# Modulation vectors from row sums of products on DVE, in a two-layer diffusion transformer block

## The chip, the cores and the metric

The kernel runs on one core of a Trainium2 chip. The metric is the device time of one execution in microseconds (us). The engines are called by the profile's names: PE does matmuls (PEld loads their stationary side), DVE is the vector engine, ACT the scalar engine, POOL is GpSimd, and SP only issues transfers. Each engine works through its own queue in order; POOL and SP also issue DMA transfers.

## The reference

Two layers work on a sequence `x` of 512 tokens and a context `xc` of 256 tokens, both 1024 wide, all in float32. Each layer begins with nine modulation vectors for `x` and nine for `xc`, which shift, scale and gate its three sub-blocks:

```
def modulation(cvec, w, b):
    m = jax.nn.silu(cvec) @ w + b
    m = m.reshape(m.shape[0], 1, N_MOD, D_MODEL)     # N_MOD 9, D_MODEL 1024
    return [m[:, :, j] for j in range(N_MOD)]

mx = modulation(c, ada_w[i], ada_b[i])               # ada_w[i] is 1024 x 9216
mc = modulation(c_ctx[None, :], ada_w[i], ada_b[i])
x = x + 0.5 * mx[2] * swiglu(pre_norm(x, norm1_g[i], mx[0], mx[1]), ...)      # FFN 1; xc alike
... pre_norm(x, norm2_g[i], mx[3], mx[4]) @ w_in[i] ...                       # four mixers
x = x + mx[5] * (jnp.concatenate([ya, yd, ym, yn], axis=-1) @ w_out[i])
x = x + 0.5 * mx[8] * swiglu(pre_norm(x, norm3_g[i], mx[6], mx[7]), ...)      # FFN 2
```

`ada_w` is 37.7 MB a layer, and each of its elements is used for two products only (one for `c`, one for `c_ctx`). In the last layer `xc` leaves after the mixers, so `mc[5]` to `mc[8]` of layer 1 are not used.

## The kernel before

Activations lie transposed, features on the partitions, tokens along the row: `A` is the 512 tokens of `x`, `C` the 256 of `xc`. Every large product is three matmuls (`mm3`: high part by high part, by low part, low by high), so a weight tile `wr` is loaded by SP, rounded by ACT to `wh` and its rest taken by DVE to `wl`; there are three buffers of each. A feed-forward (`ffn`) takes 22 blocks `f` of 128 hidden features in four groups: gate and up matmuls into `guC` (for C) and `gA`, `uA` (for A), ACT's Silu, DVE's product `h`, its split into `hh` and `hl`, and after each group the down product `dacc`. The program's parts in order of time are: the start (loads, modulation vectors 0 and 1 of layer 0, norm), FFN 1 of layer 0, the mixers, the output product `wo` and FFN 2 of layer 0, FFN 1 of layer 1, and mixers, `wo` and FFN 2 of layer 1.

Vectors 0 and 1 of layer 0 are needed at once and are matmuls against `silc` (Silu of `c` and `c_ctx`), with 32 loads of 256 KB on SP. For the other sixteen (2 to 8 of layer 0, all of layer 1), `ada` is a generator that other work steps along (`fill`). For one vector and each 128-row slice `k` of the weights, POOL's queue loads two tiles `adaw` of 128x512, and DVE multiplies each by one `silc` value per partition and adds it to an accumulator `adaacc`, for two conditions: 32 instructions a vector. The contraction then still lies over the 128 partitions. Four matmuls against a block of ones (`adasum`) add them up, ACT copies the result, four PE transposes (`adatp`) turn it into columns, and DVE adds the bias (L186). `ffn` calls `self.fill(fill)` twice in a block; FFN 1 of layer 0 steps through layer 0's vectors, FFN 2 of layer 0 through layer 1's.

The order of instructions on each engine is not the order of the code: a list scheduler with a model of durations sorts them when the program is built, and each queue then runs in that fixed order.

Of the kernel before, what the change touches and what calls it, by code (L numbers as in the profile page):

```python
# [15 lines left out]
KD = 8  # L16
# [17 lines left out]
class Net:  # L34
# [43 lines left out]
    def ffn_pools(self, st):  # L78
        e = lambda n, b, s: st.enter_context(self.tc.tile_pool(name=n, bufs=b, side=s, reuse_waits="tile"))
        self.weights(e("wp", 3, self.side_x), 1024)  # L80
        self.fs = e("fs", 2, self.side_x)
        p = e("xp", 1, self.side_o)
        self.X = {q: p.tile([128, KD, t], F32, name="x" + q) for q, t in self.T.items()}
        self.hp = e("hp", 8, self.side_o)
        self.wa = e("wa", WB, self.side_o)

    def weights(self, pool, w, sets=None):

# [39 lines left out]
    def ada(self, l):  # L128

        nc = self.nc
        load = lambda q, t, k, c: q.dma_start(out=t, in_=self.I["ada_w"][l, k * 128:(k + 1) * 128, c:c + 512])  # L133
        if l == 0:
            acc = self.psum(name="adaacc")
            for k in range(KD):
                for g in range(4):
                    w = self.hp.tile([128, 768], F32, tag=("hh", "hl")[g % 2], name="adaw")[:, :512]
                    load(nc.sync, w, k, g * 512)
                    nc.tensor.matmul(acc[32 * g:32 * g + 32, :], lhsT=self.silc[:, k], rhs=w,  # L140
                                     start=(k == 0), stop=(k == KD - 1), tile_position=(0, 32 * g))
            tp = self.ada_rows(acc)
            src = tp.rearrange("p s (g r) -> p g s r", r=32)[:, :, :, 0:2]
            self.ada_bias(l, 0, src, 4)
            self.mod_cols(l, 1)
            yield
        for j in range(2 if l == 0 else 0, 9):
            acc = [self.wa.tile([128, 512], F32, tag="acc", name="adaacc", bufs=AB) for _ in range(4)]
            for k in range(KD):
                for g in range(2):  # L150
                    w = self.wa.tile([128, 512], F32, tag="wa", name="adaw")
                    if l == 0 and j == 2 and k < WB // 2:

                        nc.gpsimd.tensor_copy(w[:, 0:1], self.XNl["A"][:, KD - 1, 0:1].bitcast(F32))
                    load(nc.gpsimd, w, k, j * 1024 + g * 512)
                    for v in range(2):
                        t, c = acc[2 * g + v], self.silc[:, k, v:v + 1]
                        if k == 0:
                            nc.vector.tensor_scalar(out=t, in0=w, scalar1=c, scalar2=None, op0=ALU.mult)  # L159
                        else:  # L160
                            nc.vector.scalar_tensor_tensor(out=t, in0=w, scalar=c, in1=t, op0=ALU.mult, op1=ALU.add)  # L161
                yield
            for _ in range(AL):
                yield
            ps = self.psum(name="adasum")
# [3 lines left out]
            src = tp.rearrange("p s (g v r) -> p g s v r", g=2, v=2)[:, :, :, :, 0]  # L169
            self.ada_bias(l, j * 8, src, 2)  # L170
            self.mod_cols(l, j)
            yield

    def ada_rows(self, acc):
        nc = self.nc
# [12 lines left out]
    def mod_cols(self, l, j):  # L188

        nc = self.nc  # L190
        i = j // 3
        src = self.mods[l][:, j * 8:(j + 1) * 8]
        if j % 3 == 1:
            g = self.gains[:, 3 * l + i].rearrange("p (k o) -> p k o", o=1).to_broadcast([128, KD, 2])
            nc.vector.scalar_tensor_tensor(out=self.modAs[l][:, i], in0=src, scalar=1.0, in1=g, op0=ALU.add, op1=ALU.mult)
        elif j % 3 == 2:
            nc.vector.tensor_scalar(out=self.modGs[l][:, i], in0=src, scalar1=1.0 if i == 1 else 0.5, scalar2=None, op0=ALU.mult)

    def fill(self, n):

        for _ in range(n):
            if next(self.side, self) is self:
                return


    def unit(self, u):
# [85 lines left out]
        nc.tensor.matmul(out, lhsT=wl, rhs=xh, start=False, stop=stop)  # L292


    def ffn(self, l, i, parts, fill=0, save=(), then=None, ns=0):

        nc = self.nc
        fi = 0 if i == 0 else 1
# [3 lines left out]
        for gi, (f0, f1) in enumerate(GROUPS):  # L302
            H = []
            for f in range(f0, f1):
                W = [self.weight(up[l, fi, f, :, j], 1024) for j in range(2)]
                hh = self.hp.tile([128, 768], F32R, tag="hh", name="hh")
                hl = self.hp.tile([128, 768], F32R, tag="hl", name="hl")
                h32 = self.fs.tile([128, 768], F32, tag="h32", name="h32")
                for p in reversed(parts):
# [12 lines left out]
                    self.fill(fill)  # L322
# [50 lines left out]
def pack(inp):  # L373
# [9 lines left out]
    r["ada_w"] = a["ada_w"]  # L383
# [955 lines left out]
class Kern(Net, Mix, DN):  # L1339

    def run(self):
# [10 lines left out]
        for l in range(2):  # L1352
# [3 lines left out]
            with ExitStack() as st:  # L1356
                self.ffn_pools(st)
                if l == 0:
                    self.load_x()
                    self.side = self.ada(0)  # L1360
                    self.fill(1)
                    self.set_layer(0)
                    for u in self.units(both, NS[0] > 0):
                        for m in range(KD):
                            self.sumsq(u, m)
                    for u in self.units(both, NS[0] > 0):
                        self.norm(u, 0)
                else:
                    self.side = self.ada(1)
                    def then(u):  # L1370
                        self.fill(80)
                        self.set_layer(1)
                        self.norm(u, 0)
                    self.second_half(0, both, then)
                def then(u):
                    self.fill(80)
                    self.norm(u, 1)
                self.ffn(l, 0, both, FILL[0] if l == 0 else 0, parts, then, NS[2 * l])
            self.mixers(l, need)
        self.open_xn()  # L1380
        with ExitStack() as st:
# [4 lines left out]
    def second_half(self, l, parts, then):  # L1386
# [62 lines left out]
                    self.norm(due, 2)  # L1449
            due = u  # L1450
        self.norm(due, 2)
        self.ffn(l, 2, parts, FILL[1] if l == 0 else 0, (), then, NS[2 * l + 1])

    def mixers(self, l, need):
        tc, nc = self.tc, self.nc
# [78 lines left out]

STEPS = 1.0
PREP, NST, LAST = (2, 3), 3, 1
FILL = (2, 3)
NK = (3, 6)

_INS = ["xT", "cxT", "cT", "ada_w", "adab", "gains", "ident", "wgu", "wd", "win", "cs_swa", "cs_mla", "sink",  # L1540
        "masks", "rpbS", "rpbT", "mlag", "wuq", "wukv", "woutk0", "woutm0", "woutk1", "woutm1", "dn_m", "dn_tri", "dn_neg", "dn_i2", "convw", "dngate", "dnng"]


# [31 lines left out]
```

## Time and profile before

| | us |
|---|---|
| median of 3 runs (3255.51 to 3258.74) | 3257.91 |
| the profiled execution | 3254.35 |
| its span, first to last instruction | 3252.6 |
| PE busy in the span | 3129.6 (96%) |
| DVE busy | 1715.9 (53%) |
| ACT busy | 1069.6 (33%) |
| POOL busy | 463.6 (14%) |
| DVE's product-and-add for the modulation (L161), 448 instructions | 315.4 |

Matmuls overlap their neighbours, so a duration in the table of groups is longer than the step from one start to the next; where the text speaks of a step it means the difference of two starts. Rows are quoted as the profile prints them; L12 is line 12 of the program.

### The profile page before, as it was taken

What the parts mean: (1) busy time and instruction counts of PE and PEld (TensorE: products, weight loads), DVE (VectorE), ACT (ScalarE), POOL (GpSimd) and SP (SyncE); (2) the same over time, 40 slices, a digit from 0 to 9 for tenths busy, and PEclk for the clock granted to TensorE, in tenths of its full rate; (3) what the DMA queues carried; (4) which work ended last, traced back from release to release, by engine and by line L of the source; (5) the groups of instructions that cost most, each with busy time, mean ns of one, the idle gap of its engine ahead of it and who ended that gap; (6) DMA issues with size and microseconds to landing.
All of it is one profiled execution on the core that took longest, in us unless ns stands there. A gap on an engine that the chain in (4) does not pass through costs nothing.

```text
span 3252.6 us, 48912 instructions
## 1 busy us (share of the span) xinstructions
PE 3129.6 (96%) x19586; PEld 2713.3 (83%) x19586; DVE 1715.9 (53%) x3044; ACT 1069.6 (33%) x1927; POOL 463.6 (14%) x772
## 2 busy tenths in 40 slices
PE   7999999998999999999999999999997899999998
PEld 4888888886788889888889988888886688788887
DVE  5746354836855477675736332322746744353334
ACT  3212112555444433121224212122455353342223
POOL 2201010411232021121102000000311322000001
PEclk9999999999999999999999999999998999899999
DMA  6534242514533354454424221212523623323333
GB/s 244 153 104 138 87 117 81 168 62 124 159 91 87 89 191 131 142 153 126 128 77 123 63 64 59 72 53 67 148 78 114 162 57 81 121 86 96 97 97 104
DMA packets 135396, 357.45 MB, mean 110 GB/s; under 512 B 20000, under 2 KB 33824, under 8 KB 134912
## 3 DMA queue, kind: packets, MB, share of 16 engines
q1 hardware_dynamic: 101056, 255.47, 25.9%
q0 software_dynamic: 34112, 98.85, 11.0%
q8 instruction: 154, 2.52, 0.3%
q14 instruction: 74, 0.61, 0.1%
HBM read 316.89 MB, written 39.65 MB: 110 GB/s over the span
## 4 chain that ended last, share of the span: by engine, by line
PE 57%; DVE 4%; issue 3%; DMA 2%; ACT 1%; POOL 0%; POOLq 0%; DVEq 0%; SPq 0%; ACTq 0%
PE dacc L290 4%; PE dacc L292 4%; PE dacc L291 4%; PE gA L290 4%; PE gA L291 4%; PE uA L290 4%; PE uA L292 4%; PE uA L291 4%; PE gA L292 4%; PE guC L292 3%; PE guC L290 3%; PE guC L291 3%; PE o L740 2%; PE pj L290 1%; PE pj L292 1%
## 5 line engine op out<-in xcount | busy, mean ns | idle before, releaser
L269 ACT CAST wh<-wr 128x1024 fp32r<-128x1024 f32 (+5 forms) x443 | 394.7, 893 | 1239.4 <-PE dacc L291 453.3
L274 DVE TENSOR_TENSOR wl<-wr,wh 128x1024 fp32r<-128x1024 f32 (+5 forms) x443 | 461.2, 1043 | 422.6 <-ACT wh L269 391.6
L290 PE MATMUL dacc<-hh,wh 128*128 128x256 f32 (+1 forms) x1392 | 452.5, 326 | 2.2 <-ACT wh L269 1.9
L292 PE MATMUL dacc<-hh,wl 128*128 128x256 f32 (+1 forms) x1392 | 450.4, 326 | 3.6 <-DVE wl L274 3.5
L291 PE MATMUL dacc<-hl,wh 128*128 128x256 f32 (+1 forms) x1392 | 452.2, 326 | 0.0
L161 DVE SCALAR_TENSOR_TENSOR adaacc<-adaw,silc,adaacc 128x512 f32<-128x512 f32 x448 | 315.4, 748 | 12.2 <-DMA adaw<-ada_w 11.8
L290 PE MATMUL guC<-xnhC,wh 128*128 128x256 f32 x1056 | 300.2, 285 | 1.6 <-ACT xnhC L263 1.5
L291 PE MATMUL guC<-xnlC,wh 128*128 128x256 f32 x1056 | 299.5, 284 | 1.5 <-DVE xnlC L264 1.5
L292 PE MATMUL guC<-xnhC,wl 128*128 128x256 f32 x1056 | 299.0, 283 | 0.5 <-DVE wl L274 0.5
L290 PEld LDWEIGHTS dacc<-hh,wh 128*128 128x128 f32 x1392 | 261.4, 188 | 32.0 <-ACT wh L269 6.1
L290 PE MATMUL gA<-xnhA,wh 128*128 128x512 f32 (+1 forms) x752 | 284.8, 379 | 1.7 <-ACT xnhA L263 1.7
L292 PEld LDWEIGHTS dacc<-hh,wl 128*128 128x128 f32 x1392 | 261.0, 188 | 29.6 <-DVE wl L274 5.0
L290 PE MATMUL uA<-xnhA,wh 128*128 128x512 f32 (+1 forms) x752 | 283.0, 376 | 0.6 <-ACT wh L269 0.6
L292 PE MATMUL uA<-xnhA,wl 128*128 128x512 f32 (+1 forms) x752 | 282.8, 376 | 0.7 <-DVE wl L274 0.7
L291 PE MATMUL uA<-xnlA,wh 128*128 128x512 f32 (+1 forms) x752 | 282.9, 376 | 0.0
L292 PE MATMUL gA<-xnhA,wl 128*128 128x512 f32 (+1 forms) x752 | 282.8, 376 | 0.0
L291 PE MATMUL gA<-xnlA,wh 128*128 128x512 f32 (+1 forms) x752 | 282.2, 377 | 0.0
L291 PEld LDWEIGHTS dacc<-hl,wh 128*128 128x128 f32 x1392 | 261.4, 188 | 24.6
L133 POOL DMA_DIRECT2D adaw<-ada_w x256 | 140.6, 550 | 799.2 <-DVE adaacc L159 483.3
L348 DVE SCALAR_TENSOR_TENSOR xA<-dacc,modG,xA 128x512 f32<-128x512 f32 (+1 forms) x160 | 101.9, 640 | 239.3 <-PE dacc L292 239.2
L290 PEld LDWEIGHTS guC<-xnhC,wh 128*128 128x128 f32 x1056 | 202.7, 192 | 9.5 <-ACT wh L269 5.2
L291 PEld LDWEIGHTS guC<-xnlC,wh 128*128 128x128 f32 x1056 | 202.6, 192 | 4.4 <-DVE xnlC L264 2.0
(354 smaller groups left out, 5944.9 us busy)
## 6 DMA issues: line engine op xcount, KB each, us to landing
wr<-wgu SPq DMA_DIRECT2D x176, 512.0 KB, 3.6
adaw<-ada_w POOLq DMA_DIRECT2D x256, 256.0 KB, 3.3
wr<-wd SPq DMA_DIRECT2D x120, 320.0 KB, 3.0
wr<-wd SPq DMA_DIRECT2D x64, 384.0 KB, 3.2
wr<-win SPq DMA_DIRECT2D x44, 512.0 KB, 3.9
adaw<-ada_w SPq DMA_DIRECT2D x32, 256.0 KB, 5.2
hl<-eh SPq DMA_DIRECT2D x32, 192.0 KB, 3.0
hl<-el SPq DMA_DIRECT2D x24, 192.0 KB, 3.3
```

The costliest lines, as they stand in the source:

```text
L133: load = lambda q, t, k, c: q.dma_start(out=t, in_=self.I["ada_w"][l, k * 128:(k + 1) * 128, c:c + 512])
L161: nc.vector.scalar_tensor_tensor(out=t, in0=w, scalar=c, in1=t, op0=ALU.mult, op1=ALU.add)
L269: nc.scalar.copy(hi, src)
L274: (nc.vector if leng == "V" else nc.gpsimd).tensor_tensor(lo, src, hi.bitcast(F32), op=ALU.subtract)
L290: nc.tensor.matmul(out, lhsT=wh, rhs=xh, start=start, stop=False)
L291: nc.tensor.matmul(out, lhsT=wh, rhs=xl, start=False, stop=False)
L292: nc.tensor.matmul(out, lhsT=wl, rhs=xh, start=False, stop=stop)
L348: nc.vector.scalar_tensor_tensor(out=x, in0=acc, scalar=gate[:, i, m, r:r + 1], in1=x, op0=ALU.mult, op1=ALU.add)
L740: nc.tensor.matmul(o[:, q0 + q], lhsT=p[:, q * 128:q * 128 + 128], rhs=v(kb), start=False, stop=kb == 3 and q == n // 128 - 1)
```

## The change

The weights come from the host transposed as well (`ada_t`: 128 output features on the partitions, the 1024 inputs along the row). `crow` holds `c` and `c_ctx` as rows; SP loads them to all 128 partitions (`silr`, 128x2x1024, 1 MB written) and ACT applies Silu. One DVE instruction then multiplies a tile of 128x1024 with one condition's row, adds up along the row, starts from the bias, and leaves 128 finished values in a column of `mod`. The sums on PE, ACT's copies, the transposes and the bias adds of the sixteen vectors go. One tile is 512 KB, with four buffers in place of six of 256 KB. `fill` now takes the share of the block that is done, and the sixteen vectors are spread over three feed-forwards: 2 to 7 of layer 0 over FFN 1 of layer 0, then 8 of layer 0 and 0 to 3 of layer 1 over FFN 2 of layer 0, then 4 to 8 of layer 1 over FFN 1 of layer 1. The unused `c_ctx` vectors 5 to 8 of layer 1 are left out, so there are 224 products. Vectors 0 and 1 of layer 0 stay matmuls. The scratch that POOL's transfers use is 4096 bytes a partition.

```diff
-WB, AB = 6, 5
-AL = 3
+AB = 4
...
+        self.silr = self.const.tile([128, 2, 1024], F32, name="silr")
+        nc.sync.dma_start(out=self.silr, in_=self.I["crow"].rearrange("(o v) k -> o v k", o=1).to_broadcast([128, 2, 1024]))
+        nc.scalar.activation(self.silr, self.silr, ACTF.Silu)
...
-                    load(nc.gpsimd, w, k, j * 1024 + g * 512)
-                    for v in range(2):
-                        t, c = acc[2 * g + v], self.silc[:, k, v:v + 1]
...
-                            nc.vector.scalar_tensor_tensor(out=t, in0=w, scalar=c, in1=t, op0=ALU.mult, op1=ALU.add)
...
-            for i in range(4):
-                nc.tensor.matmul(ps[32 * i:32 * i + 32], lhsT=self.ones[:, 0:32], rhs=acc[i], tile_position=(0, 32 * i))
-            tp = self.ada_rows(ps)
...
+        for n, (l, j) in enumerate(js):
+
+            nv = 1 if l == 1 and j >= 5 else 2
+            for m in range(j * 8, j * 8 + 8):
+                w = self.wa.tile([128, 1024], F32, tag="wa", name="adaw", bufs=AB)
+                if l == 0 and n == 0 and m - j * 8 < AB:
+
+                    nc.gpsimd.tensor_copy(w[:, 0:1], self.XNl["A"][:, KD - 1, 0:1].bitcast(F32))
+                nc.gpsimd.dma_start(out=w, in_=self.I["ada_t"][l, m])
+                for v in range(nv):
+                    o = self.wa.tile([128, 1024], F32, tag="wo", name="adao", bufs=1)
+                    nc.vector.tensor_tensor_reduce(o, w, self.silr[:, v], 1.0, self.adab[:, l, m:m + 1],
+                                                   ALU.mult, ALU.add, self.mods[l][:, m, v:v + 1])
...
-    nc = bacc.Bacc("TRN2", target_bir_lowering=False, num_devices=1)
+    nc = bacc.Bacc("TRN2", target_bir_lowering=False, num_devices=1, dynamic_dma_scratch_size=4096)
```

PE, early in FFN 2 of layer 0, where the sums of layer 1's first vector stood (about 1239 us of the profile); before:

```order
L290 MATMUL guC<-xnhC,wh 128x256
L291 MATMUL guC<-xnlC,wh 128x256
L290 MATMUL uA<-xnhA,wh 128x256
L291 MATMUL uA<-xnlA,wh 128x256
L167 MATMUL adasum<-adaacc,ones 32x512 x4
L292 MATMUL guC<-xnhC,wl 128x256
L290 MATMUL guC<-xnhC,wh 128x256
```

The same place now:

```order
L286 MATMUL guC<-xnhC,wh 128x256
L287 MATMUL guC<-xnlC,wh 128x256
L286 MATMUL uA<-xnhA,wh 128x256
L287 MATMUL uA<-xnlA,wh 128x256
L286 MATMUL guC<-xnhC,wh 128x256
```

The four sums are gone, and the feed-forward's matmuls follow one another. Of PE's 18019 instructions 128 go in all, 64 sums and 64 transposes.

DVE, from the first modulation work of FFN 1 of layer 0 on (about 64 us); before:

```order
L159 TENSOR_SCALAR adaacc<-adaw,silc 128x512 x4
L327 TENSOR_TENSOR h_410<-sg,guC 128x256
L161 SCALAR_TENSOR_TENSOR adaacc<-adaw,silc,adaacc 128x512 x2
L274 TENSOR_TENSOR wl<-wr,wh 128x1024
L161 SCALAR_TENSOR_TENSOR adaacc<-adaw,silc,adaacc 128x512 x2
L327 TENSOR_TENSOR h_410<-sg,uA 128x512
```

The same place now (each product is two instructions, the row product and the read of its sum into `mod`):

```order
L160 ISA adao,mod_72<-adaw,silr,adab 128x1024
L160 ISA mod_72 128x1
L323 TENSOR_TENSOR h_413<-sg,guC 128x256
L160 ISA adao,mod_72<-adaw,silr,adab 128x1024
L160 ISA mod_72 128x1
L270 TENSOR_TENSOR wl<-wr,wh 128x1024
L160 ISA adao,mod_72<-adaw,silr,adab 128x1024
L160 ISA mod_72 128x1
L323 TENSOR_TENSOR h_413<-sg,uA 128x512
```

Two or four short instructions ahead of a block's product or weight rest became one long and one tiny one.

DVE, at the output product `wo` of layer 0 (about 1160 us; `xC`, `xA` are the closes that free its banks); before:

```order
L274 TENSOR_TENSOR wl<-wr,wh 128x1024
L161 SCALAR_TENSOR_TENSOR adaacc<-adaw,silc,adaacc 128x512 x5
L1409 SCALAR_TENSOR_TENSOR xC<-wo,modG_76,xC 128x256
L161 SCALAR_TENSOR_TENSOR adaacc<-adaw,silc,adaacc 128x512
L1409 SCALAR_TENSOR_TENSOR xC<-wo,modG_76,xC 128x256
L274 TENSOR_TENSOR wl<-wr,wh 128x1024
```

The same place now:

```order
L270 TENSOR_TENSOR wl<-wr,wh 128x1024
L1407 SCALAR_TENSOR_TENSOR xC<-wo,modG_76,xC 128x256 x2
L270 TENSOR_TENSOR wl<-wr,wh 128x1024
L1407 SCALAR_TENSOR_TENSOR xC<-wo,modG_76,xC 128x256
L1407 SCALAR_TENSOR_TENSOR xA<-wo,modG_76,xA 128x512 x3
```

The modulation work left this stage; its first product of the second batch now stands behind the norm that follows `wo`. On SP the load of `silr` stands ahead of `adab` and of the loads of `x`; the rest of SP's order is as it was.

## Rows read from the trace of the kernel before

**Rows 1.** Busy time in four stretches (stretch, length, engines, PE clock, DMA share, GB/s).
```profile
0.00:44.00 44.00, 23.53 (x85) 6.84 (x85) 12.20 (x27) 13.90 (x24) 7.52 (x13) 0.96 0.90 338
44.00:617.00 573.00, 570.07 (x3384) 496.74 (x3384) 340.94 (x537) 145.37 (x232) 91.62 (x162) 1.00 0.41 122
...
1240.00:1780.00 540.00, 540.00 (x3255) 473.98 (x3252) 335.10 (x529) 131.09 (x208) 84.64 (x141) 1.00 0.44 129
1780.00:2345.00 565.00, 561.34 (x3430) 503.18 (x3428) 209.55 (x317) 144.44 (x233) 26.90 (x39) 1.00 0.26 76
```
**Rows 2.** PE's waits for weights' rests, 44 to 608 us: total us, times, longest.
```profile
PE dacc L292 <- DVE wl L274: 0.5, 1, 0.5
```
**Rows 3.** Order of time on PE at one sum: start, length, instruction.
```profile
1239.08 0.28 PE L291 MATMUL uA<-xnlA,wh 128*128 128x256 f32 x1
1239.29 1.06 PE L167 MATMUL adasum<-adaacc,ones 128*32 128x512 f32 x8
1240.28 0.38 PE L292 MATMUL guC<-xnhC,wl 128*128 128x256 f32 x1
1240.50 0.28 PE L290 MATMUL guC<-xnhC,wh 128*128 128x256 f32 x1
```
**Rows 4.** The same at one vector's transposes.
```profile
1248.42 0.28 PE L292 MATMUL uA<-xnhA,wl 128*128 128x256 f32 x1
1248.54 0.60 PE L180 MATMUL adatp<-ident,adasb 128*128 128x128 f32 x4
...
1249.09 0.28 PE L291 MATMUL guC<-xnlC,wh 128*128 128x256 f32 x1
```
**Rows 5.** The same at the first vector's sums, issued in four pieces.
```profile
94.81 0.39 PE L291 MATMUL uA<-xnlA,wh 128*128 128x512 f32 x1
95.03 0.39 PE L292 MATMUL uA<-xnhA,wl 128*128 128x512 f32 x1
95.35 1.05 PE L167 MATMUL adasum<-adaacc,ones 128*32 128x512 f32 x2
...
96.66 0.40 PE L291 MATMUL gA<-xnlA,wh 128*128 128x512 f32 x1
```
**Rows 6.** Groups by line on PE (count, busy us, mean ns, idle before).
```profile
L167 PE MATMUL adasum<-adaacc,ones 128*32 128x512 f32 x128 | 20.2, 605 | 0.0
L180 PE MATMUL adatp<-ident,adasb 128*128 128x128 f32 x68 | 10.2, 273 | 0.7 <-ACT adasb L177 0.7
```
**Rows 7.** Groups by line and shape on DVE.
```profile
L161 DVE SCALAR_TENSOR_TENSOR adaacc<-adaw,silc,adaacc 128x512 f32<-128x512 f32 x448 | 315.4, 748 | 12.2 <-DMA adaw<-ada_w 11.8
L274 DVE TENSOR_TENSOR wl<-wr,wh 128x1024 fp32r<-128x1024 f32 x227 | 277.8, 1226 | 319.6 <-ACT wh L269 301.2 <-PE gA L292 5.6 <-PE htr L995 4.3
L327 DVE TENSOR_TENSOR h<-sg,uA 128x512 f32<-128x512 f32 x88 | 60.4, 687 | 246.7 <-PE uA L292 246.0 <-ACT sg L326 0.7
L159 DVE TENSOR_SCALAR adaacc<-adaw,silc 128x512 f32<-128x512 f32 x64 | 28.2, 481 | 5.8 <-DMA adaw<-ada_w 4.2 <-PE adasum L167 1.5
L247 DVE TENSOR_SCALAR rsv<-nsum 128x2 f32<-128x2 f32 x20 | 3.0, 152 | 1.5 <-PE nsum L233 1.3
```
**Rows 8.** ACT's wait for a free weight buffer: total us, times, longest.
```profile
ACT wh L269 <- PE gA L291: 283.2, 77, 4.7
```
**Rows 9.** Busy time in the start, columns as in rows 1.
```profile
30.00:42.00 12.00, 11.32 (x36) 2.52 (x36) 2.99 (x3) 1.46 (x2) 0.00 (x0) 0.87 1.05 411
```
**Rows 10.** A load of 1 MB in the list of DMA issues (KB, us to landing).
```profile
xA<-xT SPq DMA_DIRECT2D x2, 1024.0 KB, 6.7
```
**Rows 11.** Order of time on DVE and PE in `wo` of layer 0.
```profile
1160.84 3.40 DVE L161 SCALAR_TENSOR_TENSOR adaacc<-adaw,silc,adaacc 128x512 f32<-128x512 f32 x5
1164.15 0.48 DVE L1409 SCALAR_TENSOR_TENSOR xC<-wo,modG,xC 128x256 f32<-128x256 f32 x1
...
1165.74 0.50 PE L290 MATMUL wo<-xnhA,wh 128*128 128x512 f32 x1 [1.29 <-DVE xC L1409]
...
1166.87 0.39 PE L292 MATMUL wo<-xnhC,wl 128*128 128x256 f32 x1 [0.40 <-DVE wl L274]
```

More of the change, by code (lines that the diff above doesn't have):

```diff
@@ L84, in ffn_pools @@
         self.hp = e("hp", 8, self.side_o)
-        self.wa = e("wa", WB, self.side_o)
+        self.wa = e("wa", 1, self.side_o)
     def weights(self, pool, w, sets=None):
@@ L132, in ada @@
         nc = self.nc
[L133 to L154, printed above, removed]
-                    load(nc.gpsimd, w, k, j * 1024 + g * 512)
-                    for v in range(2):
-                        t, c = acc[2 * g + v], self.silc[:, k, v:v + 1]
-                        if k == 0:
-                            nc.vector.tensor_scalar(out=t, in0=w, scalar1=c, scalar2=None, op0=ALU.mult)
-                        else:
-                            nc.vector.scalar_tensor_tensor(out=t, in0=w, scalar=c, in1=t, op0=ALU.mult, op1=ALU.add)
-                yield
-            for _ in range(AL):
-                yield
-            ps = self.psum(name="adasum")
-            for i in range(4):
-                nc.tensor.matmul(ps[32 * i:32 * i + 32], lhsT=self.ones[:, 0:32], rhs=acc[i], tile_position=(0, 32 * i))
-            tp = self.ada_rows(ps)
[L169 to L172, printed above, removed]
@@ new lines, in ada_first @@
+        acc = self.psum(name="adaacc")
+        for k in range(KD):
+            for g in range(4):
+                w = self.hp.tile([128, 768], F32, tag=("hh", "hl")[g % 2], name="adaw")[:, :512]
+                nc.sync.dma_start(out=w, in_=self.I["ada_w0"][k * 128:(k + 1) * 128, g * 512:(g + 1) * 512])
+                nc.tensor.matmul(acc[32 * g:32 * g + 32, :], lhsT=self.silc[:, k], rhs=w,
+                                 start=(k == 0), stop=(k == KD - 1), tile_position=(0, 32 * g))
+        tp = self.ada_rows(acc)
@@ new lines, in ada_first, with ada @@
+        src = tp.rearrange("p s (g r) -> p g s r", r=32)[:, :, :, 0:2]
+        self.ada_bias(0, 0, src, 4)
+        self.mod_cols(0, 1, 2)
+    def ada(self, js):
+        nc = self.nc
+        for n, (l, j) in enumerate(js):
[9 more added lines that the diff above has]
+                                                   ALU.mult, ALU.add, self.mods[l][:, m, v:v + 1])
+                if m == j * 8 + 7:
+                    self.mod_cols(l, j, nv)
+                yield
@@ L186, in ada_bias, with mod_cols, beside, fill @@
         self.nc.vector.tensor_tensor(dst, src, b, op=ALU.add)
-    def mod_cols(self, l, j):
+    def mod_cols(self, l, j, nv):
         nc = self.nc
         i = j // 3
-        src = self.mods[l][:, j * 8:(j + 1) * 8]
+        src = self.mods[l][:, j * 8:(j + 1) * 8, 0:nv]
         if j % 3 == 1:
-            g = self.gains[:, 3 * l + i].rearrange("p (k o) -> p k o", o=1).to_broadcast([128, KD, 2])
-            nc.vector.scalar_tensor_tensor(out=self.modAs[l][:, i], in0=src, scalar=1.0, in1=g, op0=ALU.add, op1=ALU.mult)
+            g = self.gains[:, 3 * l + i].rearrange("p (k o) -> p k o", o=1).to_broadcast([128, KD, nv])
+            nc.vector.scalar_tensor_tensor(out=self.modAs[l][:, i, :, 0:nv], in0=src, scalar=1.0, in1=g, op0=ALU.add, op1=ALU.mult)
         elif j % 3 == 2:
[L197 to L203, printed above, removed]
+            nc.vector.tensor_scalar(out=self.modGs[l][:, i, :, 0:nv], in0=src, scalar1=1.0 if i == 1 else 0.5, scalar2=None, op0=ALU.mult)
+    def beside(self, js):
+        self.side, self.sides, self.sided = self.ada(js), 8 * len(js), 0
+    def fill(self, part):
+        while self.sided < min(1.0, part) * self.sides:
+            self.sided += 1
+            next(self.side, None)
     def unit(self, u):
@@ L292, in mm3, with ffn @@
         nc.tensor.matmul(out, lhsT=wl, rhs=xh, start=False, stop=stop)
-    def ffn(self, l, i, parts, fill=0, save=(), then=None, ns=0):
+    def ffn(self, l, i, parts, save=(), then=None, ns=0):
         nc = self.nc
@@ L308, in ffn @@
                 h32 = self.fs.tile([128, 768], F32, tag="h32", name="h32")
-                for p in reversed(parts):
+                for n, p in enumerate(reversed(parts)):
                     if p == "C":
@@ L1359, in run @@
                     self.load_x()
-                    self.side = self.ada(0)
-                    self.fill(1)
+                    self.ada_first()
+                    self.beside([(0, j) for j in range(2, 8)])
                     self.set_layer(0)
@@ L1368, in run @@
                 else:
-                    self.side = self.ada(1)
+                    self.beside([(0, 8)] + [(1, j) for j in range(4)])
                     def then(u):
-                        self.fill(80)
                         self.set_layer(1)
@@ L1375, in then @@
                 def then(u):
-                    self.fill(80)
                     self.norm(u, 1)
-                self.ffn(l, 0, both, FILL[0] if l == 0 else 0, parts, then, NS[2 * l])
+                if l == 1:
+                    self.beside([(1, j) for j in range(4, 9)])
+                self.ffn(l, 0, both, parts, then, NS[2 * l])
             self.mixers(l, need)
@@ L1451, in second_half @@
         self.norm(due, 2)
-        self.ffn(l, 2, parts, FILL[1] if l == 0 else 0, (), then, NS[2 * l + 1])
+        if l == 1:
+            self.beside([])
+        self.ffn(l, 2, parts, (), then, NS[2 * l + 1])
     def mixers(self, l, need):
```

11 lines of the change are left out of this document (6 added, 5 removed).

## The prediction

> **What bounds the kernel.** I read the busy time by stretches first, then PE's waits, then the order of time on PE around the work that goes, and last the groups by line. In the three feed-forwards that carry modulation work now or after the change, PE is busy 570.07 of 573 us, 540.00 of 540 and 561.34 of 565, at a granted clock of 1.00 of 2.4 GHz [rows 1]. DVE is busy 340.94, 335.10 and 209.55 us of them, so it has 230 us to spare in the first, 205 in the second and 355 in the third. Within 44 to 608 us PE waited for a weight's rest from DVE for 0.5 us in all [rows 2]. So these stages are as long as PE's steps: an instruction taken off PE shortens them by its step, and work moved about on DVE costs nothing while weights come in time. The start is another matter: from 30 to 42 us the DMA share is full (1.05) at 411 GB/s [rows 9], and the first feed-forward begins behind these loads.
>
> **What goes from PE.** At one set of four sums, the matmuls around it start at 1239.08 and 1240.50, 1.42 us apart, with one ordinary matmul and the sums between them [rows 3]. Two ordinary steps of that shape take 0.12 us each (1248.42 to 1248.54 [rows 4]), so the set costs 1.42 - 0.24 = 1.18 us. (By busy time, 20.2 us for 128 records [rows 6], eight would be 1.26; records overlap their neighbours, so I take steps.) A vector's four transposes cost, from 1248.42 to 1249.09 with two ordinary steps in it, 0.67 - 0.24 = 0.43 us [rows 4]. The first vector of layer 0 was summed in four pieces with feed-forward matmuls between; one piece costs 96.66 - 95.03 - 2 x 0.22 = 1.19 us (a step of 512 columns is 95.03 - 94.81 = 0.22 [rows 5]), four of them 4.8 us. There are sixteen vectors (128 records of sums by 8, and 64 of the 68 transposes [rows 6]): 15 x 1.18 + 4.8 + 16 x 0.43 = 17.7 + 4.8 + 6.9 = **29.4 us off PE**. All sixteen lie in the two stages where PE has nothing to wait for, so I count all of it. Below nothing it can hardly go; the bound on this side is that PE then waits for something else (a rival below).
>
> **What DVE gets.** The trace has no row product with a sum, so I bound it. Two float32 tiles of 512 columns cost 687 ns, of 1024 columns 1226 ns, 539 for another 512; the old product with a scalar per partition costs 748 [rows 7]. One product of 1024 with such a scalar is then 748 + 539 = 1.29 us, and the read of the sum is like DVE's smallest instruction here, 0.15 [rows 7]: 1.44 us, 224 of them 323 us. The old work was 315.4 + 28.2 = 344 [rows 7], so DVE is about even. Lower bound 1.23 us; upper bound, if the stream ran at half speed, 748 + 539 + 1067 (another 1024 columns at 539 per 512 make 1.08) = 2.4, with the read 2.5. By stage: FFN 1 of layer 0 loses 28 x 0.48 + 196 x 0.75 = 160 us and gets 96 x 1.44 = 138; FFN 2 of layer 0 gets 80 x 1.44 = 115 for the larger part of 288 old instructions; FFN 1 of layer 1 gets 48 x 1.44 = 69 on top of 210, of 565. None fills.
>
> What could hurt is DVE's order: an `h`, an `hl` or a weight's `wl` queues behind a product. The cover is PE's lead. ACT mostly waits for PE to free a weight buffer, 283.2 us in 77 waits behind gate matmuls [rows 8]; from there the next up weight is needed only after 24 up matmuls of A and 24 gate matmuls of C, 24 x 0.22 + 24 x 0.12 = 8.2 us. `wl` takes 1.23 us [rows 7], ACT's rounding of the same tile I put at the same, together 2.5, so DVE may be 5.7 us late before PE feels it. Two products in front are 2.9 us now, against 1.5 us for a pair of the old ones. I take nothing for it, and 0 to 8 us as bounds; if the cover were gone, each block would lose up to 1.4 us, the difference of the pairs.
>
> [...]
>
> **The start.** `silr` is 128 x 2 x 1024 x 4 bytes = 1.05 MB ahead of the loads that bound the start; at 411 GB/s [rows 9] it moves everything behind it by **2.6 us**. All partitions read the same 8 KB, which no load here does; from below, nothing, if queues were still filling; from above, the 6.7 us that a load of 1 MB takes to land [rows 10], say 6.7. I take 2.6, since the DMA engines are the limit. ACT's Silu on `silr` comes before its squares of `x`; those are not what the stage ends with (the loads are), so I take nothing for it; it costs a few us if they were.
>
> **The output product.** In `wo` of layer 0 DVE ran five old products from 1160.84 for 3.40 us while a close of `xC` and then a `wl` stood behind them; PE idled 1.29 us for the close and 0.40 for the rest [rows 11]. Now no modulation work stands there: loads of the second batch wait for the norm behind `wo`. I take 1.5 of the 1.7 us back (bounds 0 and 2). What is late next there is the norm itself, as before.
>
> **POOL and its queue.** 128 loads of 512 KB replace 256 of 256 KB; same bytes, half the issues. In FFN 1 of layer 1 40 loads are new, 21 MB in 565 us, 37 GB/s beside 76 [rows 1], far from the 411 seen. POOL's stores of `x` come in the last group, when the products are issued. Nothing.
>
> **Sum.** -29.4 + 2.6 - 1.5 = -28.3 us. The profiled execution took 3254.35, giving 3226.1; the runs' median is 3257.91, 3.6 us above it, so I predict 3257.91 - 28.3 = **3229.6, say 3229.5 us**. Its own range is 3224 to 3235.
>
> **The rivals.**
> 1. The start is dearer, the one row read 128 times being slow: +4 us and more, 3234 to 3238. For it: no such read in the trace. Against: 1 MB loads land in 6.7 us. Chance 0.08.
> 2. [...] Chance 0.13.
> 3. The change does not do what it says: PE loses the sums but waits as long for weights, because the stage is really paced by ACT and DVE. Time 3252 to 3262. For it: DVE is at work 60% of these stages, in the same chain as the weights. Against: 0.5 us of waits [rows 2], and ACT waits for PE [rows 8], not PE for ACT. Chance 0.06.
> 4. The other side: DVE becomes the bound. In the first feed-forward its other work is 341 - 160 = 181 us, which leaves 392 for 96 products: from 4.1 us a product on, over three times my price, PE must wait. At 4.4 us it loses 96 x 0.3 = 29 us there and the gain is gone; at 5 us it loses 96 x 0.9 = 86, and the time is about 3315 even if FFN 2 loses nothing. For it: an instruction form that no row shows. Against: three rows at one column per about 1.05 ns. Chance 0.05.
> My forecast keeps 0.68.
>
> Two runs differ from no change only by more than about 0.2% (6.5 us). Forecast and rivals 1 and 2 are faster by that (0.89), rival 3 is the same (0.06), rival 4 slower (0.05). The range takes forecast, 1 and 2 with the bounds: low 3257.9 - 29.4 - 2 = 3226, less the 3.6 by which single executions lie lower and a little for the order elsewhere, 3220; high -29.4 + 6.7 + 8 = 3243.
>
> **What would show it.** Right: PE's busy time in the span falls by some 25 to 30 us; no waits over 1 us inside the feed-forwards; the first feed-forward begins 2 to 3 us later than at 44 us; products of 1.2 to 1.5 us with small reads; no modulation work on DVE in `wo`. Wrong: waits of PE for `wl` in FFN 1 of layer 0 (rival 2 or 4), a start more than 5 us later (rival 1), or other stalls in the mixers from the scheduler's new order, which I could not price and hold at a few us of either sign.

## The result

The changed kernel took **3222.69 us** (median of 4 runs, 3218.36 to 3226.16), the kernel before, on the same chip, 3256.71 (4 runs): a ratio of 0.9895, 95% interval 0.9878 to 0.9912. That is 34.0 us less, where 28.3 were forecast.

The busy time of the changed kernel by stretches, for the same stages as [rows 1] (stretch, length, then each engine, PE's granted clock, DMA share, GB/s):

```profile
0.00:46.00 46.00, 24.13 (x84) 6.64 (x84) 11.79 (x26) 15.39 (x24) 7.51 (x13) 1.00 0.93 346
46.00:604.00 558.00, 555.03 (x3283) 493.21 (x3284) 316.51 (x492) 140.78 (x222) 53.30 (x92) 0.99 0.38 117
1222.00:1759.00 537.00, 534.26 (x3210) 476.75 (x3210) 338.54 (x532) 131.87 (x207) 58.45 (x95) 1.00 0.47 145
1759.00:2323.00 564.00, 560.33 (x3429) 502.86 (x3427) 208.53 (x321) 144.88 (x234) 28.31 (x40) 1.00 0.26 77
```

PE is still the full engine, and its list is shorter; DVE's load hardly moved. Its groups by line, product and read of the sum (count, busy us, mean ns, idle before), which take the place of L161 and L159 in [rows 7]:

```profile
L160 DVE CUSTOM_DVE_ANT_0 adao<-adaw,silr,adab 128x1024 f32<-128x1024 f32 x224 | 287.1, 1282 | 11.8 <-DMA adaw<-ada_t 8.5
...
L160 DVE DVE_READ_ACCUMULATOR2_ANT mod<- 128x1 f32 x224 | 18.7, 83 | 0.0
```

A product costs 1.28 us and its read 0.08, together 1.36 where 1.44 was estimated. PE's waits in the first feed-forward of layer 0 (46 to 608 us), beside [rows 2]:

```profile
PE guC L286 <- ACT xnhC L259: 1.5, 1, 1.5
PE dacc L286 <- ACT wh L265: 1.2, 2, 0.9
PE gA L286 <- ACT xnhA L259: 0.8, 1, 0.8
PE dacc L288 <- DVE wl L270: 0.5, 1, 0.5
```

Weights' rests are as punctual as before, and the other three rows stand in the trace of before too, at 1.5, 1.7 and 0.8 us. At the start, in order of time on PE, the last transposes and the first feed-forward matmul (start, length, instruction):

```profile
44.20 0.65 PE L172 MATMUL adatp<-ident,adasb 128*128 128x128 f32 x4 [0.68 <-ACT adasb L169]
46.40 0.51 PE L286 MATMUL guC<-xnhC,wh 128*128 128x256 f32 x2 [1.55 <-ACT xnhC L259]
```

DVE's groups in `wo` of layer 0 (1128 to 1198 us) hold no product; in [rows 11] five stood in a row there:

```profile
L270 DVE TENSOR_TENSOR wl<-wr,wh 128x1024 fp32r<-128x1024 f32 (+1 forms) x12 | 11.8, 981 | 14.5 <-ACT wh L265 14.1
L1407 DVE SCALAR_TENSOR_TENSOR xA<-wo,modG,xA 128x512 f32<-128x512 f32 (+1 forms) x9 | 5.8, 660 | 12.1 <-PE wo L288 12.1
```

The table below has the length of each stage, from the start of its first matmul on PE to that of the next stage, in two traces of each kernel (the second of each comes from an experiment, `before_again` and `again`); the last columns are the difference of the two means and what the forecast said.

| stage, us | before | before_again | changed | again | difference | forecast |
|---|---|---|---|---|---|---|
| start | 43.99 | 43.86 | 46.40 | 45.36 | +2.0 | +2.6 |
| FFN 1, layer 0 | 576.58 | 578.69 | 563.83 | 563.98 | -13.7 | -14.9 |
| mixers, layer 0 | 511.85 | 515.41 | 517.38 | 513.52 | +1.8 | 0 |
| `wo`, layer 0 | 74.82 | 76.22 | 71.26 | 71.25 | -4.3 | -1.5 |
| FFN 2, layer 0 | 574.43 | 575.87 | 561.77 | 562.83 | -12.9 | -14.5 |
| FFN 1, layer 1 | 566.51 | 566.90 | 564.03 | 565.05 | -2.2 | 0 |
| mixers, layer 1 | 459.17 | 460.04 | 449.46 | 458.09 | -5.8 | 0 |
| `wo`, layer 1 | 61.74 | 61.74 | 61.20 | 61.21 | -0.5 | 0 |
| FFN 2, layer 1 | 383.50 | 382.96 | 381.28 | 381.04 | -2.1 | 0 |

### The profile page after: what moved, and what is told of

Its sections match the earlier page's. It is cut to its first block, busy times and chain, and to the rows that moved or that the text cites. A ratio compares the mean times of both kernels' runs of the same rounds, so it can differ in the third digit from the quotient of the medians.

```text
span 3216.6 us, 48071 instructions
## 1 busy us (share of the span) xinstructions
PE 3092.6 (96%) x19394; PEld 2699.5 (84%) x19394; DVE 1670.6 (52%) x2964; ACT 1061.2 (33%) x1912; POOL 391.3 (12%) x646
## 4 chain that ended last, share of the span: by engine, by line
PE 55%; DVE 3%; DMA 1%; ACT 1%; issue 1%; POOL 0%; SPq 0%; POOLq 0%; DVEq 0%; ACTq 0%
PE dacc L286 4%; PE dacc L287 4%; PE dacc L288 4%; PE uA L288 4%; PE uA L286 4%; PE uA L287 4%; PE gA L287 4%; PE gA L286 4%; PE gA L288 4%; PE guC L288 3%; PE guC L286 3%; PE guC L287 3%; PE o L738 2%; PE pj L286 1%; PE pj L288 1%; PE pj L287 1%
## 5 line engine op out<-in xcount | busy, mean ns | idle before, releaser
L160 DVE CUSTOM_DVE_ANT_0 adao<-adaw,silr,adab 128x1024 f32<-128x1024 f32 x224 | 287.1, 1282 | 11.8 <-DMA adaw<-ada_t 8.5
L288 PEld LDWEIGHTS guC<-xnhC,wl 128*128 128x128 f32 x1056 | 203.0, 192 | 1.9 <-DVE wl L270 1.5
```

The lines of the kernel that those rows point to most:

```text
L160: nc.vector.tensor_tensor_reduce(o, w, self.silr[:, v], 1.0, self.adab[:, l, m:m + 1], ALU.mult, ALU.add, self.mods[l][:, m, v:v + 1])
```

## The experiments

**1. Both kernels once more.** `again` is the changed kernel, `before_again` the kernel before, without an edit.

> The changed kernel once more, unchanged. Its one profile so far and the one of before differ by -12.8 us in the first feed-forward, -12.7 in the second feed-forward of layer 0, -3.6 in `wo` of layer 0, -2.5 in the first feed-forward of layer 1, but also by +5.5 in the mixers of layer 0 and -9.7 in those of layer 1, where the change does nothing. Theory: the feed-forwards and `wo` repeat within 1 us, because their length is PE's list of steps, and the mixers move by several us from one execution to the next. Rival: the mixers repeat too, within 1 us; then their -4.2 in sum belongs to the change, by the scheduler's new order. Time 3218 to 3227.

> The kernel before once more, unchanged, for a second trace. Theory (the mixers vary from one execution to the next and the feed-forwards do not): feed-forwards at 576.6, 574.4, 566.5 within 1 us, `wo` of layer 0 at 74.8 within 0.5, the last feed-forward at 383.5; the mixers of the two layers differ from 511.9 and 459.2 by several us, as they did between executions of the changed kernel (517.4 and 513.5; 449.5 and 458.1). Rival: the mixers repeat within 1 us.

`again` took 3226.16 us (4 runs, 3215.75 to 3228.68) against 3258.11, ratio 0.990 (0.988 to 0.992); the one run of `before_again` took 3263.44. In the table the feed-forwards repeat within about 2 us, `wo` within 1.4, and the mixers move by up to 8.6 (449.46 to 458.09). So the mixers' -5.8 and +1.8 are not to be read as the change's work. PE's granted clock differs with them in the mixers of layer 1, in two traces of one and the same kernel: first the changed kernel (stage 449.46 us, mean clock 0.93), then `again` (458.09, 0.90), by stretches as above:

```profile
2728.00:2736.00 8.00, 5.09 (x77) 4.33 (x75) 3.37 (x12) 2.16 (x5) 2.65 (x4) 1.00 0.31 74
2736.00:2747.00 11.00, 9.12 (x26) 6.03 (x27) 6.03 (x12) 3.31 (x6) 1.62 (x2) 0.53 0.60 195
2747.00:2753.00 6.00, 5.22 (x35) 4.39 (x34) 4.23 (x6) 2.98 (x7) 0.00 (x0) 1.00 0.81 254
2753.00:2768.00 15.00, 13.90 (x54) 11.67 (x55) 6.01 (x13) 6.07 (x11) 0.00 (x0) 0.54 0.13 44
```

```profile
2728.00:2738.00 10.00, 9.01 (x104) 8.04 (x103) 3.77 (x13) 3.48 (x7) 1.00 (x2) 1.00 0.33 87
2738.00:2772.00 34.00, 30.45 (x118) 24.67 (x108) 17.39 (x35) 11.85 (x20) 3.26 (x4) 0.51 0.39 124
```

In both the clock falls to its lower level (0.53, 0.54 and 0.51 in these rows) after a stretch in which PE was busy 64% and 90% of the time. At that level PE's steps are longer: in the trace of before, matmuls of 128x512 start 0.427 us apart at a clock of 0.50 (2489 to 2493 us) and 0.227 apart at 1.00 (94 to 95 us). In the first of the two it comes back after 10 us and falls once more for 14; in `again` it stays down for 34. So a mixer stage can differ by 9 us with nothing changed.

**2. The sums on PE left out, alone** (with the copy on ACT, the transposes and the bias add that follow them; the old products stay).

```diff
-            ps = self.psum(name="adasum")
             for i in range(4):
-                nc.tensor.matmul(ps[32 * i:32 * i + 32], lhsT=self.ones[:, 0:32], rhs=acc[i], tile_position=(0, 32 * i))
-            tp = self.ada_rows(ps)
-            src = tp.rearrange("p s (g v r) -> p g s v r", g=2, v=2)[:, :, :, :, 0]
-            self.ada_bias(l, j * 8, src, 2)
+                g, v = i // 2, i % 2
+                nc.vector.tensor_tensor(self.mods[l][:, j * 8 + 4 * g:j * 8 + 4 * g + 4, v], acc[i][:, 0:4],
+                                        self.adab[:, l, j * 8 + 4 * g:j * 8 + 4 * g + 4], op=ALU.add)
```

> The kernel before with the four sums on PE of each vector, their copy on ACT and the four transposes left out; what the vectors get instead is the unsummed product of each partition in four of its columns plus the bias, so the modulation vectors are not what the reference computes. All old products and loads stay, in their old order. Theory (PE's steps are the stage's length): 29.4 us less than before, ratio 0.991, with about -14.5 to -15 in each of the two feed-forwards of layer 0 and `wo` as before. Rival (the stage is paced by the weights' rest on DVE and PE's time does not carry): within 5 us of before. Second rival (sums cost more than their steps, by what they disturb around them): -34 or more.

It took 3272.20 us against 3258.11, ratio **1.0048** (1.0033 to 1.0063): slower, which neither expectation had. The first feed-forward did get shorter (564.6 us), but `wo` of layer 0 grew to 84.2 and the second feed-forward to 599.8. PE's waits from 1119 to 1275 us, the end of `wo` and the norm behind it, and the busy time in three stretches from there:

```profile
PE gA L289 <- DVE xnlA L262: 12.7, 6, 2.3
PE gA L288 <- ACT xnhA L261: 10.9, 7, 2.6
PE rb L238 <- DVE dg L234: 7.4, 1, 7.4
PE guC L288 <- ACT xnhC L261: 4.7, 2, 3.8
PE guC L289 <- DVE xnlC L262: 2.5, 1, 2.5
```

```profile
1119.00:1203.00 84.00, 73.32 (x469) 66.57 (x468) 64.28 (x105) 21.39 (x37) 30.11 (x43) 0.94 0.68 218
1203.00:1271.00 68.00, 40.37 (x221) 36.54 (x222) 68.00 (x141) 13.25 (x28) 21.83 (x39) 0.80 0.49 146
1271.00:1803.00 532.00, 529.68 (x3170) 472.05 (x3170) 281.17 (x448) 131.01 (x205) 59.16 (x95) 1.00 0.36 108
```

DVE is busy all of 68 us, PE only 40 of them, and the granted clock falls to 0.80. All five rows wait for pieces of a norm that stand behind products on DVE (48 of L161 in this `wo`, 30 in that of before). Before, an accumulator came free only when PE had summed it (L159 waits for `adasum` in [rows 7]), and the sums had their place among the feed-forward's matmuls. So I read the sums as what paced DVE: without them the products moved forward in DVE's order, into `wo` and the norm. That the move comes from this, and not from another reason for which the scheduler sorted anew, is argued; experiment 4 tests what the move costs.

**3. The changed kernel without its second gate.** In the changed kernel the first four loads of the first two batches each wait, by a small POOL copy, for the norm's `XNl`. Here only those of the first batch do.

```diff
-                if l == 0 and n == 0 and m - j * 8 < AB:
+                if l == 0 and n == 0 and j == 2 and m - j * 8 < AB:
```

> The changed kernel with the second batch's first four loads no longer tied to the norm behind `wo`, so that the first products of that batch run in `wo` of layer 0 as the old ones did. Theory (modulation work on DVE in front of closes and weights' rests costs PE waits there): `wo` of layer 0 goes from 71.3 back towards the 74.8 us of the kernel before, +1.5 to +3.5, the rest unchanged. Rival (the 3.6 us there come from the order of `wo` and the norm, not from the products): `wo` stays within 0.5 us of 71.3.

It took 3253.53 us (10 runs), ratio 0.9987 (0.9977 to 0.9997), 27.4 more than `again` on the same chip: without the gate the change gains 4.6 us. `wo` went to 77.1 and the second feed-forward to 577.7, so the expectation had the sign and the place, and the size far too small. PE's waits from 1134 to 1240 us:

```profile
PE guC L286 <- ACT xnhC L259: 5.9, 2, 4.6
PE guC L287 <- DVE xnlC L260: 2.7, 2, 2.2
PE nsum L229 <- DVE nt L256: 1.3, 1, 1.3
```

They name the same norm. The first row names ACT, whose `xnhC` needs `nt` from DVE. The rows add up to 9.9 us, of 21 that these two stages lost; from 1208 to 1233 us the granted clock has a mean of 0.73, and how the rest divides is open.

**4. The gate in the kernel before, without and with its sums.** `no_sums_gated` is experiment 2, `gate_only` the kernel before, each with

```diff
-                    if l == 0 and j == 2 and k < WB // 2:
+                    if j == (0 if l else 2) and k < WB // 2:
```

> As the earlier kernel without the sums on PE (the vectors again get the unsummed product of each partition in four of its columns plus the bias, so they are not what the reference computes), and in addition the first three loads of layer 1's vectors wait for the norm behind `wo`, as the changed kernel's second batch does. Theory (the sums on PE also paced DVE: without them the old products crowd into `wo` and stand ahead of closes and the norm; a gate mends that, and what is left is PE's own time): `wo` of layer 0 at 71.3 us instead of 84.2, the second feed-forward at 561 to 563 instead of 599.8, the time 27 to 33 us less than before, ratio 0.990 to 0.992. Rival (the loss came from something else in that kernel, such as the small bias operations, or a product of the old kind is too slow without pacing wherever it begins): `wo` 71 to 75, but the second feed-forward stays above 580 and the time within 10 us of before.

> The kernel before, sums on PE kept, with the one addition that the first three loads of layer 1's vectors wait for the norm behind `wo`. Theory: `wo` of layer 0 falls from 74.8 to about 71.3 us, the second feed-forward stays at 574, so 3 to 4 us less in all, ratio 0.999. Rival (the gate delays the vectors so that the end of layer 0 waits for the last one): the second feed-forward or the start of the first one of layer 1 grows by 5 us or more.

`no_sums_gated` took 3236.29 us against 3257.15, ratio 0.9931 (0.9913 to 0.9949): with the gate, leaving PE's work out pays 20.9 us, `wo` is 71.26 and the first feed-forward 562.2, but the second stays at 571.1, between the two expectations. PE's steps on `gA` in it (each from one start to the next, added up) are 131.1 us against 121.7 before, so 9.4 us of what is missing lie there. `gate_only` took 3264.75, ratio 1.0015 (0.9996 to 1.0034), which can't be told from no change: `wo` fell to 71.28 as the theory had it, and the second feed-forward grew to 591.1, as the rival had it, but not for the rival's reason: matmul by matmul against the trace of before, all of the 16.6 us are lost in the first 47 us of the stage, and nothing at its end. Most of it is lost at A's norm, where DVE is full and PE's clock falls (the stretch from 1232 to 1256 us, columns as above):

```profile
1232.00:1256.00 24.00, 16.62 (x75) 14.95 (x74) 24.00 (x39) 6.45 (x10) 6.98 (x13) 0.57 0.64 186
```

DVE's order of time there, first in `gate_only`, then in the changed kernel:

```profile
1230.37 0.48 DVE L264 SCALAR_TENSOR_TENSOR xnlA<-nt,mod,xnhA 128x256 fp32r<-128x256 f32 x1
1230.76 2.73 DVE L161 SCALAR_TENSOR_TENSOR adaacc<-adaw,silc,adaacc 128x512 f32<-128x512 f32 x4
1233.41 0.47 DVE L260 SCALAR_TENSOR_TENSOR nt<-xA,modA,rb 128x256 f32<-128x256 f32 x1
1233.80 0.48 DVE L264 SCALAR_TENSOR_TENSOR xnlA<-nt,mod,xnhA 128x256 fp32r<-128x256 f32 x1
1234.20 2.73 DVE L161 SCALAR_TENSOR_TENSOR adaacc<-adaw,silc,adaacc 128x512 f32<-128x512 f32 x4
```

```profile
1222.19 0.87 DVE L256 SCALAR_TENSOR_TENSOR nt<-xA,modA,rb 128x256 f32<-128x256 f32 x2
1222.97 1.28 DVE L160 CUSTOM_DVE_ANT_0 adao<-adaw,silr,adab 128x1024 f32<-128x1024 f32 x1
1224.18 0.08 DVE L160 DVE_READ_ACCUMULATOR2_ANT mod<- 128x1 f32 x1
1224.18 0.87 DVE L260 SCALAR_TENSOR_TENSOR xnlA<-nt,mod,xnhA 128x256 fp32r<-128x256 f32 x2
```

A's norm is written in two halves of its columns, and the gate opens on a column of the first. In the second half four old products (2.73 us) stand ahead of each slice, its `nt` and its `xnlA`; of the new ones, two for two slices, 1.36 us a slice. PE's matmuls on A take these slices one after another, so the old bunch stalls them: their steps on `gA` are 131.1 us in `gate_only` too, and 124.5 in the changed kernel.

**5. The gate on the norm's last column.** `late_gate` is the changed kernel with that, in both batches; `late_gate_old` is `gate_only` with it for layer 1's vectors alone.

```diff
-                    nc.gpsimd.tensor_copy(w[:, 0:1], self.XNl["A"][:, KD - 1, 0:1].bitcast(F32))
+                    nc.gpsimd.tensor_copy(w[:, 0:1], self.XNl["A"][:, KD - 1, TX - 1:TX].bitcast(F32))
```

> The kernel before with the sums on PE kept and the first loads of layer 1's vectors tied to the last column of the norm of A (the earlier gate was its first column, which is written by the first of the norm's two column halves, so that four old products of 0.7 us stood between the pieces of the second half). Theory (the 16.6 us that the second feed-forward lost under the earlier gate were those products in front of `xnlA`, and the half clock that followed PE's waits): no product inside that norm, `wo` at 71.3, the second feed-forward at 572 to 575, the time 3 to 6 us under before, ratio 0.998 to 0.999. Rival (the loss came from the vectors being late or dense over the whole stage): the second feed-forward stays above 585.

> The changed kernel with its gate on the last column of A's norm in place of the first, in both batches. Theory (the new products in the second half of that norm cost gA steps some 2 to 3 us: 124.5 us of gA steps in the second feed-forward against 121.7 before): the second feed-forward at 559 to 561 instead of 562.4, gA steps at 121.7, the time 1 to 4 us under the changed kernel's. Rival (those waits come from the norm itself): gA steps stay at 124.5 and the time does not change.

`late_gate` took 3223.31 us against 3254.84, ratio 0.9905 (0.9886 to 0.9924). Its second feed-forward is 558.9 us, and PE's steps on `gA` in it are 121.5 us, against 124.5 in the changed kernel and 121.7 before: the theory's 3 us are there in the trace, but the whole time can't show them beside the mixers (527.3 in this trace, with 41 us at the lower clock). `late_gate_old` took 3270.51, ratio 1.0044 (1.0029 to 1.0058), so the theory failed: no product is left inside the norm, and the second feed-forward still takes 594.6. The rival had the size (above 585) and half of the reason: the vectors are late, but not over the whole stage. One row of PE's waits (1195 to 1795 us) holds 15.4 of the 20 us by which it is longer than before:

```profile
PE adasum L168 <- DVE adaacc L162: 15.4, 1, 15.4
```

The first vector's sum has its fixed place in PE's order; when the products begin later, PE stands there until DVE has added up the vector. With sums on PE the products are bound from both sides: early, they hold up the norm; late, PE waits for them. The row products end in `mod`, and PE has no place that waits for them soon.

**6. The start.** The load of `silr` and its Silu go behind the first norm, on POOL's queue.

```diff
-        nc.sync.dma_start(out=self.silr, in_=self.I["crow"].rearrange("(o v) k -> o v k", o=1).to_broadcast([128, 2, 1024]))
-        nc.scalar.activation(self.silr, self.silr, ACTF.Silu)
...
+        if js and js[0] == (0, 2):
+            nc.gpsimd.tensor_copy(self.silr[:, 0, 0:1], self.XNl["A"][:, 3, 0:1].bitcast(F32))
+            nc.gpsimd.dma_start(out=self.silr, in_=self.I["crow"].rearrange("(o v) k -> o v k", o=1).to_broadcast([128, 2, 1024]))
+            nc.scalar.activation(self.silr, self.silr, ACTF.Silu)
```

> The changed kernel with the load of `silr` (1.05 MB read from one 8 KB row pair into all partitions) moved from SP's queue ahead of the `x` loads to POOL's queue behind the first norm, ahead of the products' own loads. Theory (the start pays for 1.05 MB at 411 GB/s): the first feed-forward begins 2.4 us earlier, at about 44.0 us, and the time falls by 2 to 2.5 us from that of the changed kernel. Rival (the start ends with ACT's or SP's chain, not with the bytes): less than 1 us. A second effect could take it back: the products begin some 5 us later and bunch, with stalls of PE for a weight's rest in the first column blocks.

> The changed kernel with the later gate and with the load of `silr` behind the first norm on POOL's queue. Theory: start 2 to 2.5 us earlier than the changed kernel's, second feed-forward 1 to 3 us shorter, so 3 to 5 us under it, near 3219 to 3222 as a median. Rival (the products begin later and bunch): the feed-forwards of layer 0 grow by as much.

The first feed-forward began at 43.29 and 43.28 us, against 46.40 and 45.36 in the changed kernel: 2.1 to 3.1 us, as the load's bytes had it. The edit moves the Silu of `silr` too (1.91 us on ACT), but in the changed kernel ACT stood idle 10.56 us near the end of the start, for sums on PE, whose own operands waited 24 times, 11.9 us in all, for loads of `adaw`; so the Silu is not what the stage ends with:

```profile
43.55 0.59 ACT L169 COPY adasb<-adaacc 128x512 f32<-128x512 f32 x1 [10.56 <-PE adaacc L138]
```

The whole took 3221.26 (ratio 0.9898, 0.9879 to 0.9916) alone and 3221.01 (0.9890, 0.9872 to 0.9907) with the later gate, whose second feed-forward was 558.4. Both stages are shorter in the traces, and the first feed-forward is not longer (563.4 and 564.6); that the whole is faster than the changed kernel the runs can't show.

**7. The products two and four times** (`range(4)` in `x4_products`).

```diff
-                    nc.vector.tensor_tensor_reduce(o, w, self.silr[:, v], 1.0, self.adab[:, l, m:m + 1],
-                                                   ALU.mult, ALU.add, self.mods[l][:, m, v:v + 1])
+                    for _ in range(2):
+                        nc.vector.tensor_tensor_reduce(o, w, self.silr[:, v], 1.0, self.adab[:, l, m:m + 1],
+                                                       ALU.mult, ALU.add, self.mods[l][:, m, v:v + 1])
```

> The changed kernel with every row product issued twice, the second writing the same values again: 2 x (1.28 + 0.08) = 2.7 us in front of whatever waits on DVE, where the forecast's bound for a product was 2.5 us. Theory (150 us of spare DVE time and a lead of 5.7 us for an up weight): the first feed-forward of layer 0 gets 96 x 1.36 = 131 us more on DVE, 444 of 564, and stays within 3 us of 564; the second, which is the fullest (DVE 93% busy in its first 240 us), runs its products longer but also stays within 5 us; the time is at most 8 us above that of the changed kernel. Rival (products stand in bunches of up to six ahead of one weight's rest): 16 us in a bunch against a lead of 5.7, each bunch costs PE several us, the two feed-forwards of layer 0 grow by 20 us or more each.

> The changed kernel with every row product issued four times, each writing the same values: 5.46 us in place of 1.36. Theory (the forecast's point of balance is 4.1 us a product): DVE becomes the bound of the first feed-forward of layer 0, 181 + 96 x 5.46 = 705 us against 564, so it grows by about 140 us; the second, with 80 products of its batch (437 us of them) and about 150 us of its own, stands at 587 against 562, +25 us or more, since the products also bunch; the first of layer 1 has 48 products (262 us on top of 210) and does not fill. Together 3225 + 140 + 25 = 3390, 3350 to 3420. Rival (two products already cost nothing, and the order gives so much cover that PE is touched only in part): under 3300.

Twice costs nothing: 3224.90 us, ratio 0.9908 (0.9883 to 0.9932), feed-forwards of layer 0 at 563.6 and 562.0. Busy time by stretches in these two, as for the changed kernel above:

```profile
46.00:604.00 558.00, 554.52 (x3286) 492.87 (x3287) 433.33 (x685) 140.71 (x222) 53.73 (x93) 1.00 0.38 117
1222.00:1754.00 532.00, 529.44 (x3173) 472.19 (x3173) 488.23 (x778) 129.97 (x204) 57.19 (x94) 1.00 0.48 145
```

DVE is busy 488 of 532 us, and PE still 529. Four times cost 3397.37, ratio 1.0433 (1.0407 to 1.0459); the sum expected was 3390. The place was wrong: the first feed-forward grew by only 26 us (589.8), the second by 23 (584.5), the first of layer 1 by 14 (578.1), and the mixers of layer 0 by about 110 (626.7). That the total came near the sum expected is luck. DVE's busy time from 635 to 760 us, of L161's products and reads alone, and the longest wait of PE from 600 to 1262:

```profile
635.00:760.00 125.00, 102.66 (x159) 0.63 0.24 73
```

```profile
PE pj L287 <- DVE ab L1491: 86.2, 1, 86.2
```

DVE's fixed order let PE run ahead through the feed-forward: there PE waited 2.8 us for weights' rests, and its one long wait, 15.4 us, is for a close of `xC`. The products that were left over stood in a row ahead of the mixers' first piece of work, `ab`.

## Why the prediction came out

**The likeliest case came true.** 3222.69 lies in the range 3220 to 3243, 1.3 us below the forecast's own range of 3224 to 3235. That it is so near is in part luck. In the table the four stages that the forecast priced give -28.9 us for its -28.3, but only because the feed-forwards fall short of it by 2.8 us and `wo` goes beyond it by 2.8. PE's busy time fell by 37 us (3129.6 to 3092.6), more than the 25 to 30 that the forecast named as its sign.

**PE's steps.** A set of sums repeats in the trace of before at 0.996 us from its first start to the next matmul, and the matmuls beside it take about 0.1 us longer each; that is the 1.18 of the forecast. At a granted clock of 1.00 a step of 512 columns takes 0.107 us more than one of 256 (0.227 against 0.120), 2.4 columns a ns; if one column is counted to a clock, that gives an estimate of 2.4 GHz for the full clock, as in the forecast. What the two feed-forwards gave is 26.6 us, not 29.4. In the second, five products inside A's norm took 2.8 us back on `gA`; with the later gate that stage gives 16.2 and 16.8 (575.15 to 558.92 and 558.40), more than the 14.5 of the sums. Steps on `guC` also fell, from 131.7 to 128.0 us, 2.8 of it in the stage's first 28 us. No product stands in C's norm in either kernel; but behind the products in `wo` DVE of before began C's `nt` 1.1 us ahead of the stage's first matmul, where the changed kernel has 3.5. In the first 1.2 us are missing. In the traces the steps on `nsum`, for the norm at the stage's end, are 1.0 us longer (1.9 to 2.9 and 2.8); why is open.

**DVE.** Price and cover held: 1.36 us a product, and a pair twice as long in front of a weight's rest cost nothing. The doubled products, 2.7 us, go past the upper bound of 2.5 without a loss, so rival 2, products of 2.5 us that make DVE slip where they bunch, falls in its effect as well as in its price. The upper bound's stream at half speed was the author's estimate, and it does not show for this product with a running sum: 1282 ns for 1024 columns, against 1226 for the plain difference of the same size in [rows 7]. The 8 us that the range adds for stalls behind products no run shows either: with the doubled products the feed-forwards of layer 0 take 563.6 and 562.0 us, where the changed kernel has 563.83 and 561.77. Rival 4's price shows in the fourfold run: at 5.46 us a product DVE does hold PE up, but most of the loss lies behind the stage that the forecast named.

**The start.** Mis-sized by little: +2.0 for +2.6, and shown by moving the load away.

**The output product is the term that was mis-sized, and its reason was too narrow.** The forecast said rightly that "no modulation work stands there" and gave it 1.5 us, read from two waits. `wo` gave 4.3, above the bound of 2, and that is the small part. The same gate kept the products out of C's norm and the first half of A's, which open the second feed-forward, and without it the kernel is 27 us slower. In before, that norm was free of products with the sums on PE; the forecast priced their removal only as PE time, and experiment 2 shows that removal alone to be a loss of 14 us. Without the gate the time would have been the one that rival 3 gave (3252 to 3262; experiment 3 took 3253.53), though not by its reason: the waits there name the norm, not the weights. The forecast's total holds because the change has both parts, the row products and the gate.

**What was put at nothing.** The first feed-forward of layer 1 and the last one gained 2.2 and 2.1 us, in both traces; that the scheduler's new order did it is argued only. All stages of these traces together give -37.7 us, and -8.8 of it lies where the forecast put nothing, -4.0 of that in the mixers, which is within what they vary.

## What to carry to other kernels

An instruction that is taken off the bounding engine may also have paced another one (experiment 2 took 14 us more): ask what its result or its freed buffer held back, and what that engine will run early. Work on an engine with spare time can still cost where it stands ahead of the short chains at a stage's border (here the norm, 27.4 us in experiment 3), so try a gate of its loads on the end of that chain; and work whose result goes to the bounding engine at a fixed place could here be neither early (steps on `gA` of 131.1 us in `gate_only`, against 121.7) nor late (a wait of 15.4 us in `late_gate_old`). Compare stages, not only totals: here a feed-forward repeats to about 2 us while the whole moves by 10.

## What was not expected of the hardware

The granted clock's stay at its lower level differs from one execution to the next of the same kernel: in the mixers of layer 1 it is 34 us in `again`, where the first trace of that kernel has 10 and 14 with 7 at full speed between. In the mixers of layer 0, behind about 1070 to 1090 us, it is 14 us in ten traces and 37 to 44 us in three (`ungated`, `late_gate`, `late_rows`; the fourfold run is left aside), with mixers of 511 to 517 us and of 524 to 527 us. Why, no run shows; each of the three is the only trace of its kernel, so that the kernel has a part in it there can't be ruled out. In experiment 2 stalls of PE and a lower clock came together: the waits of the table above add up to 38 us, and the granted clock in the 68 us around them is 0.80. How much the longer steps of the matmuls between add to the waits, no run separates.
